# Tiles of SBUF moved to addresses that are multiples of 128 bytes, in a one-core attention and FFN layer

## The chip, the cores and the metric

One core of one Trainium2 chip runs the whole layer in one launch. The metric is the device time of that core in microseconds. TensorE (PE) multiplies, VectorE (DVE), ScalarE (ACT) and GpSimd (POOL) do the rest, and all transfers are issued by SyncE (SP). Working data lies in SBUF, where a tile has 128 partitions and the same byte range in each of them; "address" below means the first byte of that range. Matrix products land in PSUM.

## The reference, cut to what matters

One layer over 1,024 latent tokens and 256 context tokens, width 1,024, all in float32: modulated RMS norm, one input projection, two attention mixers that read the same input, one output projection, and a SwiGLU FFN of hidden width 2,816.

```
h  = _modulate(_rms_norm(x, norm1_g), sh1, sc1);  hc = _modulate(_rms_norm(ctx, norm1_g), csh1, csc1)
q_a, k_a, v_a, q_b, k_b, v_b = _in_proj(h, w_in)          # and the same for hc
o_a = _window_gqa_latent(q_a, k_a, v_a, k_ac, v_ac, sink_a)
o_b = _neighbourhood_latent(q_b, k_b, v_b, k_bc, v_bc, rpb_b)
x_new = x + g1 * _merge(o_a, o_b, on_a, on_b, w_out)
h2 = _modulate(_rms_norm(x_new, norm2_g), sh2, sc2)
x  = x_new + g2 * ((silu(h2 @ w_gate) * (h2 @ w_up)) @ w_down)
```

## The kernel before, in words

Every large product is made of three matmuls, since each operand is split into a high part (the value rounded to float32r, written by ACT) and a low part (the rest, by DVE or POOL): high times high, high times low, low times high, summed in one PSUM tile. One operand of a matmul is the moving one (512 columns here, 2,048 bytes of each partition), the other the stationary one (128 columns, 512 bytes), loaded into PE ahead of the matmul.

The stages, in order of time:

- **Input projection** (`gemm_k`, lines 246 to 248). Moving: the split weights `whi`, `wlo`. Stationary: the split input, `hTh` and `hl` for the eight latent row blocks, `hcTh` and its own `hl` tiles for the two context blocks. Key and value columns come first, the queries are mixed into the attention.
- **Attention A and B** (`scores`, `a_front`, `a_back`, `b_front`, `b_back`): score matmuls at line 452, softmax on DVE, ACT and POOL (line 494 scales the weights `P` by `den`), transposes at lines 506 and 636, copies of them into `PT` by ACT (lines 511, 641) and DVE (509, 639). The **output projection** is spread over B (`out_proj`, lines 809 to 811; moving `wo`, stationary `oh` and `ol`).
- **FFN, gate and up** (`group`, `prod`, lines 977, 979, 980). A 2x2 block scheme with seven products. Stationary: the split weight combinations `fwhl`. Moving: one of seven split combinations of the activations, `B11`, `B21`, `BT3`, `BT1`, `BT2`, `B22`, `BT4`, each with a high and a low tile (`h`, `l` at the end of the name).
- **FFN, down** (`dprod`, `dmm`, line 1188). Both operands are `dhl` tiles, of which there are 24; ACT and DVE split them from `draw` tiles just loaded (lines 114 and 117).

Each engine runs its instructions in the order in which the built program has them. Tiles come from pools. A pool lies at the left end of SBUF, behind the pools still open there, or (`side="right"`) at the right end, in front of the pools open there. Within a pool the tiles follow each other in the order of their first use, each rounded up to a multiple of 32 bytes. So one small tile moves everything behind it in its pool, and everything on the far side of its pool.

The left end begins at byte 1,152: 1,024 bytes that `kernel` sets aside (`dynamic_dma_scratch_size=1024`) and four constants of 32 bytes. The first left pool is `cons`, with the constants. It is released after the output projection, so that the pool `f1b` (with `BT1`, `BT2`, `B22`, `BT4`) and later `dn` (with `dhl`) start at 1,152. The right end is at byte 229,344. The pool `h` (`hTh`, then the `hl` tiles) ends there, and later the FFN's pool `fw`, in front of which stand `f1a` (`B11`, `B21`, `BT3`) and `fwh` (`fwhl`).

Of the kernel before, what the change touches and what calls it, by code (L numbers as in the profile page):

```python
# [5 lines left out]
F32 = mybir.dt.float32  # L6
# [7 lines left out]
D = 1024  # L14
SEQ = 1024
CTX = 256
HD = 64
# [31 lines left out]
XTE = (0, 2)  # L49
KTE = (0,)  # L50
WOG = (0, 2)
TEN = "GVV"


# [4 lines left out]
def block(tc, d, out, dbg=()):  # L59
# [4 lines left out]
    def pool(name, bufs=1, space=None, side=None):  # L64
        kw = {}
        if space is not None:
            kw["space"] = space
        if side is not None:
            kw["side"] = side
        return tc.alloc_tile_pool(name=name, bufs=bufs, reuse_waits="tile", **kw)  # L70


    cons = pool("cons")
    ident = cons.tile([128, 128], F32, name="ident")
    load(ident, d["ident"])
    ones = cons.tile([128, 128], F32, name="ones")
    V.memset(ones, 1.0)
    mhalf = cons.tile([128, 8], F32, name="mhalf")
    V.memset(mhalf, -0.5)
    col = cons.tile([128, 72], F32, name="col")  # L80
# [2 lines left out]
    sh1 = cons.tile([128, 8, 2], F32, name="sh1")  # L83
    a2 = cons.tile([128, 8], F32, name="a2")
    sh2 = cons.tile([128, 8], F32, name="sh2")
    g1 = cons.tile([128, D], F32, name="g1")
    sr = cons.tile([128, SEQ], F32, name="sr")
    rs = cons.tile([128, 2, 8], F32, name="rs")
    sink = cons.tile([128, 8], F32, name="sink")
    load(sink, d["sink_a"].to_broadcast([128, 8]))  # L90
    nsink = cons.tile([128, 8], F32, name="nsink")
    V.tensor_scalar(nsink, sink, -1.0, None, ALU.mult)

    dram = pool("scratch", space=DRAM)
# [8 lines left out]
    f_d = dram.tile([7, NJ // 2, 128, 512], F32, name="f_d")  # L103
    t_d = dram.tile([4, NJ // 2, 128, 512], F32, name="t_d")

    def rstd_of(p, ss, n, k, name):
        r = p.tile([128, k], F32, name=name, bufs=2)
        G.tensor_scalar(r, ss, 1.0 / n, EPS, ALU.mult, ALU.add)
        G.tensor_tensor(r, r, mhalf[:, :k], op=ALU.pow)
        return r  # L110
# [13 lines left out]
    def low(p, k, dt, name):  # L124

        if p < 2:
            return hp.tile([128, 512], dt, name=name, tag="hl", bufs=HLB)
        return hcp.tile([128, CTX], dt, name=name, tag="hcl", bufs=9)
# [25 lines left out]
    wk = pool("wk0", bufs=3, side="right")  # L154
# [5 lines left out]
    T.transpose(pcol[:, :72], vrow, ident[:72, :72])  # L160
    V.tensor_copy(col, pcol[:, :72])
    S.activation(sil, col[:, 0:16], AF.Silu)
    bsc = cons.tile([128, 8], F32, name="bsc")
    V.tensor_scalar(bsc, col[:, 24:32], 1.0, None, ALU.add)
    silw = wk.tile([128, 8, 32], F32, name="silw", bufs=1)
    V.memset(silw, 0.0)
    V.tensor_copy(silw[:, :, 0:2], sil.rearrange("p (s k) -> p k s", s=2))
    sel = wk.tile([128, 2], F32, name="sel", bufs=1)
    load(sel, d["sel"])

    xT = {}
# [1 line left out]
    def load_x(i):  # L173
        xt = wk.tile([128, D], F32, name=f"x{i}", tag="in", bufs=XB)
        load(xt, d["x"][i * 128:(i + 1) * 128] if i < 8 else d["ctx"][(i - 8) * 128:(i - 7) * 128])
        ss = wk.tile([128, 1], F32, name="ss")
        S.activation(sr, xt, AF.Square, accum_out=ss)
        r = rstd_of(wk, ss, D, 1, "rx")
        V.tensor_scalar(xt, xt, r, None, ALU.mult)
        p, m = divmod(i, 4)  # L180
        if m == 0:
            xT[p] = [low(p, k, F32, f"xT{p}{k}") for k in range(8)]
        for half in range(2):
            pt = ps1.tile([128, 512], F32, name="ptx", tag="tr", bufs=2)
            for c in range(4):
                T.transpose(pt[:, c * 128:(c + 1) * 128],
                            xt[:, (4 * half + c) * 128:(4 * half + c + 1) * 128], ident)
            for c in range(4):
                dst = xT[p][4 * half + c][:, m * 128:m * 128 + 128]
                if c in XTE:  # L190
                    V.tensor_copy(dst, pt[:, c * 128:(c + 1) * 128])
                else:
                    S.activation(dst, pt[:, c * 128:(c + 1) * 128], AF.Copy)
# [65 lines left out]
        for m in range(NF):  # L259
            gemm_k(pgs[m], m, dd, ws[dd], 512)  # L260

    gkb = cons.tile([128, 2, HD], F32, name="gkb")
    for j, nm in enumerate(("qn_b", "kn_b")):
        load(gkb[:, j], d[nm].to_broadcast([128, HD]))
    V.scalar_tensor_tensor(gkb[:, 0], gkb[:, 0], 0.125, gkb[:, 1], ALU.mult, ALU.mult)
# [3 lines left out]
    for c in XO:  # L269
        if c < 10:  # L270
            load_x(c)
            if c == 3:
                h_kb(0)
            continue
        mods(c - 10)
        if c > 10:
            h_kb(c - 10)
# [165 lines left out]
    at = pool("at", bufs=2)  # L443

    def scores(segs, lh, ll):
        s = psA.tile([128, 1024], F32, name="s", tag="s", bufs=2)
        for n_, l in enumerate((lh, ll)):
            for o, rhs, n in segs:
                ov = s[:, o:o + n]
                if len(rhs.shape) == 3:  # L450
                    ov = ov.rearrange("p (r c) -> p r c", c=rhs.shape[2])
                T.matmul(ov, l, rhs, start=n_ == 0, stop=n_ == 1)  # L452
        return s

    def geo(i):
        b0, b1 = max(i - 1, 0), min(i + 1, 7)
        nl = (b1 - b0 + 1) * 128
        if i == 7:
            return b0, nl, 512, 256, 256, 0, [8, 9] + list(range(b0, b1 + 1))
        return b0, nl, 512 - nl, 512, 512 - nl, 256 + 384 - nl, list(range(b0, b1 + 1)) + [8, 9]  # L460
# [9 lines left out]
    def a_front(i, g, Ps, QT):  # L470
        QTh, QTl = QT
        b0, nl, lo_o, cx_o, s0, m0, blocks = geo(i)
        n = nl + CTX
        nm = at.tile([128, 4], F32, name="nm", bufs=3)
        den = at.tile([128, 4], F32, name="den", bufs=3)
        for h in range(4):
            hh = 4 * g + h
            s = scores([(lo_o, KTa[:, g, b0 * 128:b0 * 128 + nl], nl),
                        (cx_o, KTa[:, g, SEQ:SEQ + CTX], CTX)],
                       QTh[:, h * 128:(h + 1) * 128], QTl[:, h * 128:(h + 1) * 128])  # L480
            P = at.tile([128, 640], F32, name="P", bufs=10)
            V.tensor_tensor_reduce(P[:, :n], s[:, s0:s0 + n], mska[:, m0:m0 + n], -1.0,  # L482
                                   nsink[:, hh:hh + 1], ALU.add, ALU.min, nm[:, h:h + 1])
            S.activation(P[:, :n], P[:, :n], AF.Exp, scale=-1.0, bias=nm[:, h:h + 1],  # L484
                         accum_out=den[:, h:h + 1])
            Ps.append(P)
            yield
        es = at.tile([128, 4], F32, name="es", bufs=3)
        V.tensor_tensor(es, nm, sink[:, 4 * g:4 * g + 4], op=ALU.add)
        S.activation(es, es, AF.Exp)  # L490
        V.tensor_tensor(den, den, es, op=ALU.add)
        V.reciprocal(den, den)  # L492
        for h in range(4):
            G.tensor_scalar(Ps[h][:, :n], Ps[h][:, :n], den[:, h:h + 1], 1.0, ALU.mult, ALU.mult)  # L494
# [100 lines left out]
    def b_front(hp_, C, Ps, QT, bias):  # L595
        QTh, QTl = QT
        KT = kvs[hp_]
        nm = atb.tile([128, 4], F32, name="nm", bufs=3)
        den = atb.tile([128, 4], F32, name="den", bufs=3)
        for R in range(2):  # L600
            r0 = 4 * R
            for h in range(2):
                j = 2 * R + h
                kl = KT[h][:, :SEQ].rearrange("p (r c) -> p r c", c=64)[
                    :, r0:r0 + 12, C0S[C]:C0S[C] + 32]
                kc = KT[h][:, SEQ:]
                if R == 0:
                    s = scores([(256, kc, 256), (512, kl, 384)], QTh[:, j], QTl[:, j])
                    s0, m0 = 256, 384
                else:  # L610
                    s = scores([(128, kl, 384), (512, kc, 256)], QTh[:, j], QTl[:, j])
                    s0, m0 = 128, 0
                P = atb.tile([128, 640], F32, name="P", bufs=PBB)
                V.tensor_tensor_reduce(P, s[:, s0:s0 + 640], bias[h][:, m0:m0 + 640], -1.0,  # L614
                                       3.0e38, ALU.add, ALU.min, nm[:, j:j + 1])
                S.activation(P, P, AF.Exp, scale=-1.0, bias=nm[:, j:j + 1],  # L616
                             accum_out=den[:, j:j + 1])
                Ps.append(P)
                yield
        V.reciprocal(den, den)  # L620
        for j in range(4):
            G.tensor_scalar(Ps[j], Ps[j], den[:, j:j + 1], 1.0, ALU.mult, ALU.mult)  # L622
# [94 lines left out]
    for u in range(16):  # L717
# [18 lines left out]
        if u == UR:  # L736
# [3 lines left out]
            atb = pool("at2", bufs=2, side="right")  # L740
# [35 lines left out]
    def load_wo(grp):  # L776
        ws = []
        for c in range(4):
# [6 lines left out]
            r = col[:, 64 + 4 * grp + c:65 + 4 * grp + c]  # L785
            if c in WOG:
                G.tensor_scalar(raw, raw, r, 1.0, ALU.mult, ALU.mult)
# [124 lines left out]
    fw = pool("fw", side="right")  # L912
# [2 lines left out]
    ones2 = fw.tile([128, 128], F32, name="ones2", bufs=1)  # L915
    V.memset(ones2, 1.0)
    acc2 = fw.tile([128, 512], F32, name="acc2", bufs=1)
    sil2 = fw.tile([128, 8], F32, name="sil2", bufs=1)
    V.tensor_copy(sil2, sil[:, 0:8])
    B = {}  # L920
    for nm_ in ("11", "21", "T3"):
# [206 lines left out]
    E = {"V": V, "G": G}  # L1128
    TE = [E[x] for x in TEN]
    for k in range(4):  # L1130
# [125 lines left out]
    dn.release()  # L1256
    fw.release()
    psT.release()
    dram.release()


# [89 lines left out]
```

## Time and profile before

| | |
|---|---|
| three runs | 1409.66, 1413.19, 1413.55 us; median 1413.19 us |
| the profiled execution's own time | 1412.19 us |
| its span (first to last instruction) | 1410.4 us, so 1.8 us lie outside |
| mean granted TensorE clock | 0.975 |
| busy: PE, DVE, POOL, ACT | 1318.8, 935.8, 615.3, 598.1 us |
| transfers | 250.20 MB in 192,228 packets, 177 GB/s over the span |

Times are microseconds from the first instruction, means of one instruction are nanoseconds. A matmul's duration includes its way through the pipelined array, so that matmuls of 390 ns follow each other every 0.23 us: the rate is read from the starts. After "idle before" stands how long the engine stood idle just before instructions of that group, and what ended it.

### The profile page before, as it was taken

The page shows a single profiled execution, that of the slowest core. Times are in us where ns is not written, and L with a number is a line of the kernel's source. Part 1 is how long each engine was busy: PE and PEld are TensorE (multiplying, and loading weights), DVE is VectorE, ACT ScalarE, POOL GpSimd, SP SyncE. Part 2 cuts the span into 40 slices and gives each one's busy share as a digit, 9 for nine tenths or more (in the row PEclk, how much of TensorE's full clock was granted, in tenths as well). Part 3 has the DMA queues.
Part 4 walks back from the last instruction along what each step waited for, and adds up shares of the span by engine and source line. Part 5 has one row for each costly group of instructions (what it writes and reads, how often), then busy time and mean ns, then how long its engine had stood idle before and what let it go on. Part 6 is the DMA issues. An engine that isn't in the chain of part 4 may idle for free. (4 is left out here: it accounts for less than half of the span.)

```text
span 1410.4 us, 19052 instructions
## 1 busy us (share of the span) xinstructions
PE 1318.8 (94%) x6537; PEld 1020.5 (72%) x6537; DVE 935.8 (66%) x1533; ACT 598.1 (42%) x1200; POOL 615.3 (44%) x541
## 2 busy tenths in 40 slices
PE   6989988999998799999987889999999997999998
PEld 3668866766655477677765678888888886888886
DVE  4687775577555555566558877867777764857762
ACT  4555323554455444455644423333333331744430
POOL 1377555342122434565435686666666753000000
PEclk8999999999998899999989999999999999999999
DMA  9635364265236865556386355555555443975832
GB/s 278 212 133 196 99 171 100 73 187 186 90 99 191 218 216 188 208 166 216 112 239 217 112 189 178 175 170 169 179 187 179 156 165 129 388 281 198 279 105 59
DMA packets 192228, 250.20 MB, mean 177 GB/s; under 512 B 44604, under 2 KB 115460, under 8 KB 192004
## 3 DMA queue, kind: packets, MB, share of 16 engines
q1 hardware_dynamic: 192132, 248.99, 55.6%
q8 instruction: 51, 0.84, 0.3%
q14 instruction: 45, 0.37, 0.1%
HBM read 182.10 MB, written 66.85 MB: 177 GB/s over the span
## 5 line engine op out<-in xcount | busy, mean ns | idle before, releaser
L1188 PE MATMUL pf<-dhl 128*128 128x512 f32 x924 | 212.1, 392 | 7.1 <-DVE dhl L117 7.1
L1188 PEld LDWEIGHTS pf<-dhl 128*128 128x128 f32 x924 | 175.0, 189 | 44.1 <-DVE dhl L117 7.6
L248 PE MATMUL pg<-whi,hl 128*128 128x512 f32 (+1 forms) x368 | 134.9, 378 | 1.8 <-POOL hl L117 1.8
L117 DVE TENSOR_TENSOR dhl<-draw,dhl 128x512 fp32r<-128x512 f32 x154 | 101.8, 707 | 49.5 <-ACT dhl L114 49.4
L114 ACT ACTIVATE dhl<-draw 128x512 fp32r<-128x512 f32 x154 | 87.9, 624 | 107.2 <-PE pf L1188 75.4
L246 PE MATMUL pg<-whi,hTh 128*128 128x512 f32 (+1 forms) x320 | 122.9, 384 | 7.8 <-ACT qc L323 6.5
L117 DVE TENSOR_TENSOR fwhl<-fs,fwhl 128x512 fp32r<-128x512 f32 x88 | 101.2, 1159 | 37.6 <-ACT fwhl L114 35.2
L247 PE MATMUL pg<-wlo,hTh 128*128 128x512 f32 (+1 forms) x320 | 121.3, 379 | 0.0
L494 POOL TENSOR_SCALAR P<-P,den 128x640 f32<-128x640 f32 (+1 forms) x64 | 51.6, 827 | 119.3 <-DVE den L492 74.4
L939 POOL TENSOR_TENSOR fs<-fraw 128x512 f32<-128x512 f32 x44 | 62.5, 1424 | 78.9 <-DMA fraw<-in_w_up_dram 32.1
L248 PEld LDWEIGHTS pg<-whi,hl 128*128 128x128 f32 x368 | 69.8, 191 | 14.3 <-POOL hl L117 2.5
L114 ACT ACTIVATE fwhl<-fraw 128x512 fp32r<-128x512 f32 x58 | 36.7, 632 | 100.1 <-PE pf L980 98.4
L114 ACT ACTIVATE fwhl<-fs 128x512 fp32r<-128x512 f32 x88 | 54.8, 626 | 55.8 <-PE pf L980 54.2
L246 PEld LDWEIGHTS pg<-whi,hTh 128*128 128x128 f32 x320 | 61.2, 191 | 21.3 <-ACT qc L323 8.1
L117 DVE TENSOR_TENSOR fwhl<-fraw,fwhl 128x512 fp32r<-128x512 f32 x58 | 71.5, 1233 | 0.7 <-ACT fwhl L114 0.3
L622 POOL TENSOR_SCALAR P<-P,den 128x640 f32<-128x640 f32 x64 | 51.5, 825 | 43.9 <-DVE den L620 28.5
L247 PEld LDWEIGHTS pg<-wlo,hTh 128*128 128x128 f32 x320 | 61.3, 192 | 9.5
L484 ACT ACTIVATE P<-P,nm 128x640 f32<-128x640 f32 (+1 forms) x64 | 51.0, 798 | 39.8 <-DVE nm L482 39.7
L482 DVE CUSTOM_DVE_ANT_0 P<-s,mska,nsink 128x640 f32<-128x640 f32 (+1 forms) x64 | 52.4, 846 | 18.3 <-PE s L452 16.1
L813 POOL TENSOR_TENSOR xa<-xa,xt 128x512 f32<-128x512 f32 x28 | 40.8, 1461 | 47.2 <-DVE xa L812 38.6
L616 ACT ACTIVATE P<-P,nm 128x640 f32<-128x640 f32 x64 | 52.7, 825 | 16.1 <-DVE nm L614 16.0
L506 PEld LDWEIGHTS pt<-ident,P 128*128 128x128 f32 x304 | 34.0, 141 | 31.1 <-issue 24.4
(296 smaller groups left out, 3451.9 us busy)
## 6 DMA issues: line engine op xcount, KB each, us to landing
draw<-f_d SPq DMA_DIRECT2D x35, 512.0 KB
bt<-in_bias_b_dram SPq DMA_DIRECT2D x16, 1024.0 KB
wraw<-in_w_mod_dram SPq DMA_DIRECT2D x48, 256.0 KB
fraw<-in_w_gate_dram SPq DMA_DIRECT2D x22, 512.0 KB
fraw<-in_w_up_dram SPq DMA_DIRECT2D x22, 512.0 KB
wr<-in_w_down_dram SPq DMA_DIRECT2D x22, 512.0 KB
f_d<-sc SPq DMA_DIRECT2D x44, 256.0 KB
t_d<-wt SPq DMA_DIRECT2D x44, 256.0 KB
```

The lines of the kernel that those rows point to most:

```text
L114: S.activation(hi, src, AF.Copy)
L117: lo_eng.tensor_tensor(lo, src, f(hi), op=ALU.subtract)
L246: T.matmul(pg[:, :n], l, w[0][:, :n], start=k == 0, stop=False)
L247: T.matmul(pg[:, :n], l, w[1][:, :n], start=False, stop=False)
L248: T.matmul(pg[:, :n], hl[m // 4, k][:, m % 4 * 128:m % 4 * 128 + 128], w[0][:, :n], start=False, stop=k == 7)
L482: V.tensor_tensor_reduce(P[:, :n], s[:, s0:s0 + n], mska[:, m0:m0 + n], -1.0, nsink[:, hh:hh + 1], ALU.add, ALU.min, nm[:, h:h + 1])
L484: S.activation(P[:, :n], P[:, :n], AF.Exp, scale=-1.0, bias=nm[:, h:h + 1], accum_out=den[:, h:h + 1])
L494: G.tensor_scalar(Ps[h][:, :n], Ps[h][:, :n], den[:, h:h + 1], 1.0, ALU.mult, ALU.mult)
L616: S.activation(P, P, AF.Exp, scale=-1.0, bias=nm[:, j:j + 1], accum_out=den[:, j:j + 1])
L622: G.tensor_scalar(Ps[j], Ps[j], den[:, j:j + 1], 1.0, ALU.mult, ALU.mult)
L939: G.tensor_tensor(t, x, y, op=op_)
L1188: T.matmul(pd[t], a[:, x, l], b[:, y], start=start and i == 0, stop=stop and i == 2, skip_group_check=True)
```

## The change

The first part is a 96-byte pool that is opened on the right before all others and released last. `EDGE` is 24 float32. The second part reorders the constants, so that the large ones (`ident`, `ones`, `g1`, `sr`, `gkb`) come before the small ones; `bsc` and `gkb` move up to the others, and `nsink` takes 64 bytes. The third part pads small tiles in the other pools (`sel`, `ss`, `rx`, `nm`, `den`, `es`, `sil2`) to 128 or 64 bytes, and instructions use the first columns.

```diff
+EDGE = 24
...
+    edge = pool("edge", side="right")
+    edge.tile([128, EDGE], F32, name="edge")
     cons = pool("cons")
     ident = cons.tile([128, 128], F32, name="ident")
     load(ident, d["ident"])
     ones = cons.tile([128, 128], F32, name="ones")
     V.memset(ones, 1.0)
+    g1 = cons.tile([128, D], F32, name="g1")
+    sr = cons.tile([128, SEQ], F32, name="sr")
+    gkb = cons.tile([128, 2, HD], F32, name="gkb")
...
-    nsink = cons.tile([128, 8], F32, name="nsink")
+    bsc = cons.tile([128, 8], F32, name="bsc")
+    nsink = cons.tile([128, 16], F32, name="nsink")[:, :8]
...
-    def rstd_of(p, ss, n, k, name):
-        r = p.tile([128, k], F32, name=name, bufs=2)
+    def rstd_of(p, ss, n, k, name, room=8):
+        r = p.tile([128, room], F32, name=name, bufs=2)[:, :k]
...
-    sel = wk.tile([128, 2], F32, name="sel", bufs=1)
+    sel = wk.tile([128, 32], F32, name="sel", bufs=1)[:, :2]
...
-        ss = wk.tile([128, 1], F32, name="ss")
+        ss = wk.tile([128, 32], F32, name="ss")[:, :1]
         S.activation(sr, xt, AF.Square, accum_out=ss)
-        r = rstd_of(wk, ss, D, 1, "rx")
+        r = rstd_of(wk, ss, D, 1, "rx", 16)
...
-        nm = at.tile([128, 4], F32, name="nm", bufs=3)
-        den = at.tile([128, 4], F32, name="den", bufs=3)
+        nm = at.tile([128, 32], F32, name="nm", bufs=3)[:, :4]
+        den = at.tile([128, 32], F32, name="den", bufs=3)[:, :4]
...
-    sil2 = fw.tile([128, 8], F32, name="sil2", bufs=1)
+    sil2 = fw.tile([128, 32], F32, name="sil2", bufs=1)[:, :8]
...
     psT.release()
+    edge.release()
     dram.release()
```

No instruction is added, removed or moved: on all five engines the built program has the same instructions in the same order, and only addresses and a few waits differ. The waits follow from addresses, since a new tile waits for whatever used its bytes last. On ACT one write of `whi` loses a wait for a transfer and the first write of `BT1h` a wait for ACT itself. On POOL four writes of `wlo` wait for other earlier users, and one scaling of `P` (line 494, 512 columns) waits for PE besides ACT.

Of the 2,097 allocations of SBUF in the built program, 502 lie at a multiple of 128 before, and 2,016 after; the other 81 are small ones (`hss`, `hr`, `rx`, `xss` and constants). For the operands of the 512-column matmuls, this is where they lie, as the address modulo 512 bytes. Each slice of an operand steps by a multiple of 512 bytes, so one number stands for all of its slices.

```
pair (moving, stationary)             line            before       after        distance: before, after
whi/wlo, hTh and its hl               246 to 248      352, 480     256, 384     128   128
whi/wlo, hcTh and its hl              246 to 248      352, 352     256, 384       0   128
wo, oh/ol                             809 to 811      352, 352     384, 384       0     0
B11/B21/BT3, fwhl                     977, 979, 980   448, 448     256, 256       0     0
BT1/BT2/B22/BT4, fwhl                 977, 979, 980   128, 448     128, 256     320   128
dhl, dhl                              1188            128, 128     128, 128       0     0
```

The distance is stationary minus moving, modulo 512. Modulo 128 the distances of the six pairs are 0, 0, 0, 0, 64, 0 before and all 0 after.

## Rows read from the trace of the kernel before

**Rows 1.** The page's head: busy time of each engine, share of the span, instructions.
```profile
span 1410.4 us, 19052 instructions
PE 1318.8 (94%) x6537; PEld 1020.5 (72%) x6537; DVE 935.8 (66%) x1533; ACT 598.1 (42%) x1200; POOL 615.3 (44%) x541
```
**Rows 2.** Busy time by stretch; columns: length, PE, PEld, DVE, ACT, POOL, clock, DMA share, GB/s.
```profile
0.00:35.00 35.00, 21.62 (x123) 13.79 (x124) 15.43 (x44) 15.43 (x38) 5.29 (x14) 0.85 0.97 278
126.00:412.00 286.00, 273.83 (x1425) 204.62 (x1424) 185.87 (x412) 122.44 (x275) 118.20 (x134) 0.99 0.43 124
412.00:726.00 314.00, 287.90 (x1747) 211.85 (x1746) 178.52 (x373) 154.67 (x331) 137.35 (x144) 0.96 0.63 192
726.00:1184.00 458.00, 438.54 (x1866) 349.91 (x1867) 339.73 (x360) 161.56 (x278) 290.69 (x192) 0.99 0.52 171
1184.00:1410.00 226.00, 212.58 (x927) 175.17 (x926) 146.99 (x227) 91.81 (x163) 8.24 (x5) 0.98 0.63 220
```
**Rows 3.** Timeline of PE, down stage: start, length, engine, line, tiles, count.
```profile
1209.74 30.54 PE L1188 MATMUL pf<-dhl 128*128 128x512 f32 x134
```
**Rows 4.** Timeline of PE, FFN: first matmul of each k-run, one per row.
```profile
1000.52 0.39 PE L977 MATMUL pf<-B21h,fwhl 128*128 128x512 f32 x1
...
1001.90 0.39 PE L977 MATMUL pf<-B21h,fwhl 128*128 128x512 f32 x1
...
1003.26 0.39 PE L977 MATMUL pf<-B22h,fwhl 128*128 128x512 f32 x1
...
1006.06 0.39 PE L977 MATMUL pf<-BT4h,fwhl 128*128 128x512 f32 x1
...
1008.86 0.39 PE L977 MATMUL pf<-B11h,fwhl 128*128 128x512 f32 x1
```
**Rows 5.** Timeline of PE, input projection: context blocks, then latent blocks.
```profile
93.04 0.40 PE L248 MATMUL pg<-whi,hl 128*128 128x512 f32 x1
93.28 0.40 PE L246 MATMUL pg<-whi,hcTh 128*128 128x512 f32 x1
...
108.18 0.39 PE L248 MATMUL pg<-whi,hl 128*128 128x512 f32 x1
...
113.62 0.39 PE L248 MATMUL pg<-whi,hl 128*128 128x512 f32 x1
...
193.09 0.39 PE L248 MATMUL pg<-whi,hl 128*128 128x512 f32 x1
...
199.85 0.40 PE L247 MATMUL pg<-wlo,hTh 128*128 128x512 f32 x1
```
**Rows 6.** Groups by line and form: matmuls of the FFN and of the context blocks.
```profile
L1188 PE MATMUL pf<-dhl 128*128 128x512 f32 x924 | 212.1, 392 | 7.1 <-DVE dhl L117 7.1
L977 PE MATMUL pf<-BT4h,fwhl 128*128 128x512 f32 x88 | 34.8, 395 | 3.7 <-DVE p L1086 3.7
L979 PE MATMUL pf<-B22l,fwhl 128*128 128x512 f32 x88 | 34.7, 394 | 0.0
L980 PE MATMUL pf<-B21h,fwhl 128*128 128x512 f32 x88 | 34.3, 389 | 0.0
L246 PE MATMUL pg<-whi,hcTh 128*128 128x512 f32 x32 | 13.3, 415 | 3.1 <-ACT qc L323 3.1
```
**Rows 7.** Groups by line and form: copies into PT, in attention A and B.
```profile
L641 ACT ACTIVATE PT<-pt 128x512 f32<-128x512 f32 x48 | 28.5, 594 | 49.3 <-PE pt L636 49.2
L511 ACT ACTIVATE PT<-pt 128x512 f32<-128x512 f32 x44 | 26.2, 595 | 52.9 <-PE pt L506 52.9
L509 DVE COPY PT<-pt 128x512 f32<-128x512 f32 x32 | 22.0, 687 | 26.0 <-PE pt L506 26.0
L639 DVE COPY PT<-pt 128x512 f32<-128x512 f32 x32 | 21.9, 686 | 11.5 <-PE pt L636 11.3
```
**Rows 8.** Groups by line and form: POOL instructions whose waits differ.
```profile
L494 POOL TENSOR_SCALAR P<-P,den 128x512 f32<-128x512 f32 x16 | 11.8, 760 | 13.6 <-ACT P L484 7.9 <-DVE den L492 5.7
L117 POOL TENSOR_TENSOR wlo<-wraw,whi 128x512 fp32r<-128x512 f32 x16 | 22.8, 1437 | 6.7 <-ACT whi L114 6.6
```

More of the change, by code (lines that the diff above doesn't have):

```diff
@@ L85, in block @@
     sh2 = cons.tile([128, 8], F32, name="sh2")
-    g1 = cons.tile([128, D], F32, name="g1")
-    sr = cons.tile([128, SEQ], F32, name="sr")
     rs = cons.tile([128, 2, 8], F32, name="rs")
@@ L162, in block @@
     S.activation(sil, col[:, 0:16], AF.Silu)
-    bsc = cons.tile([128, 8], F32, name="bsc")
     V.tensor_scalar(bsc, col[:, 24:32], 1.0, None, ALU.add)
@@ L260, in h_kb @@
             gemm_k(pgs[m], m, dd, ws[dd], 512)
-    gkb = cons.tile([128, 2, HD], F32, name="gkb")
     for j, nm in enumerate(("qn_b", "kn_b")):
@@ L487, in a_front @@
             yield
-        es = at.tile([128, 4], F32, name="es", bufs=3)
+        es = at.tile([128, 32], F32, name="es", bufs=3)[:, :4]
         V.tensor_tensor(es, nm, sink[:, 4 * g:4 * g + 4], op=ALU.add)
@@ L597, in b_front @@
         KT = kvs[hp_]
-        nm = atb.tile([128, 4], F32, name="nm", bufs=3)
-        den = atb.tile([128, 4], F32, name="den", bufs=3)
+        nm = atb.tile([128, 32], F32, name="nm", bufs=3)[:, :4]
+        den = atb.tile([128, 32], F32, name="den", bufs=3)[:, :4]
         for R in range(2):
```

## The prediction

> **What bounds the kernel now.** I read the head of the page first: PE is busy for 1318.8 of 1410.4 us, and no other engine is above 66% [rows 1]. The split by stretch then tells where this holds. In the FFN's gate and up stage PE is busy for 438.54 of 458 us, in the down stage for 212.58 of 226, in the stretch of projections and attention from 126 to 412 us for 273.83 of 286, from 412 to 726 us for 287.90 of 314; only the first 35 us belong to the transfers, with a DMA share of 0.97 against 21.62 us of PE [rows 2]. A busy PE is not yet PE at its peak, so the third view is PE's timeline, for the rate at which matmuls start. The reader should see that one shape, 128x512, starts at two rates at a granted clock of 0.98 to 0.99, the 2.4 GHz level.
>
> **Two rates.** In the down stage 134 matmuls take 30.54 us; less 0.39 us for the last one's pipeline this is 30.15 over 133 intervals, 226.7 ns [rows 3]. In the FFN the twelve matmuls with `B22` and the twelve with `BT4` start from 1003.26 to 1008.86 us: 5.60 us over 24, 233.3 ns. Just before, the last six with `B21` take from 1001.90 to 1003.26: 226.7 ns; the first six take 1.38 us, 230 ns [rows 4]. Same line, same weights, no wait: only the moving tile differs, and with it the address. `B21` lies at distance 0 from `fwhl` modulo 512, `B22` and `BT4` at 320.
>
> The input projection gives the third case. The context blocks (distance 0) run 24 intervals from 108.18 to 113.62 us, 226.7 ns; the latent blocks (distance 128) run 29 from 193.09 to 199.85 us, 233.1 ns [rows 5]. So in these rows a pair at distance 0 settles at 226.7 ns, and pairs at 320 and at 128 both run at about 233. That the pair at 128 is slow is the row to hold on to: modulo 128 its distance is already 0.
>
> **The change part by part.** It adds no instruction, so every term is an old one at a new address. Each is worked out against the profiled execution's 1412.19 us, which is 1.0 us below the median of the runs.
>
> 1. *FFN, the four pairs `BT1`, `BT2`, `B22`, `BT4`.* 4 names x 3 lines x 88 = 1056 matmuls [rows 6]. Their distance goes from 320 to 128. No row shows distance 128 in this stage. The bounds are 226.7 ns (the fast rate of rows 3 to 5) and 240 ns (the slowest start-to-start step at distance 128, from 93.04 to 93.28 us [rows 5]). That is 1056 x -6.6 = -7.0 us to 1056 x +6.7 = +7.1 us. I take 233.1, the latent blocks' mean, since they are the only pair in the trace with this very distance: 1056 x -0.2 = **-0.2 us**. PE is the bound of this stage, so the term counts in full.
> 2. *Context blocks.* Their distance goes from 0 to 128. With 512 columns these are 32 matmuls at each of three lines [rows 6], 96 in all, from 226.7 to 233.1 ns: **+0.6 us**. Bounds 0 and 96 x 13.3 = +1.3 us. Part of it lies in front of waits for ACT's `qc` (3.1 us of idle before them), so 0.6 is rather too much.
> 3. *Pairs whose distance stays.* Latent blocks (128), `dhl` (924 matmuls, 0), `B11`, `B21`, `BT3` (792 matmuls, 0), `wo` with `oh` and `ol` (0). **0.** If they change after all, it is by their slow start behind another pair, 230 instead of 226.7 ns over six matmuls, 20 ns each time [rows 4]; at 66 runs this bounds the term at 1.3 us either way.
> 4. *ACT, DVE and POOL.* `PT` lies at a multiple of 128 in attention A and 96 past one in B. ACT writes it in 595 and 594 ns, DVE in 687 and 686 [rows 7]: one part in 600, in favour of neither. **0.** What hides even that is the wait for the transposes (49.2 to 52.9 us of ACT's idle); without that cover, 1 ns x 156 copies is 0.2 us.
> 5. *Transfers.* Only where DMA is the bound can this count, in the first 35 us with 278 GB/s at a share of 0.97 [rows 2]. Per unit of share that is 287 GB/s, against 220/0.63 = 349 in the down stage. If the whole difference came from addresses, the 35 us would shrink by 6 us; I see no row in which it does, and the first stretch has other packet sizes. I take **0**, with -1.5 us (a quarter of that bound) as what could come unseen, and nothing above 0, because no transfer gets a longer run or a later place in its queue. Later transfers hide under PE.
> 6. *Waits.* Four `wlo` writes on POOL and one `P` scaling get other waits. The engine's idle time before these groups is ended by ACT or DVE and not by PE or a transfer (6.6 of 6.7 us, and 7.9 + 5.7 of 13.6 us) [rows 8]; an extra wait on something already done costs nothing. One `P` scaling that did wait would hold up three more of 0.76 us. **0**, bounds -0.5 and +1. The two waits lost on ACT stood beside ones that stay.
>
> Sum: 1412.19 - 0.2 + 0.6 = **1412.6 us**.
>
> **A page of the Trainium skill that speaks against the change.** At 32-byte multiples every tile already starts on a whole line of the 16 bytes that the Trainium skill names ("SBUF — State Buffer", Operand start alignment and Door 1), and the page calls start alignment a matter of legality, not of speed. By that page terms 1 and 2 are 0 and the sum is 1412.2 us. The trace agrees with it for ACT and DVE [rows 7], but not for PE, whose two rates the page does not know [rows 4, 5].
>
> **Rivals.**
>
> *A. The distance counts modulo 128, not modulo 512.* Then the change brings every pair to 0, and the 1056 matmuls of term 1 run at 226.7 ns: -7.0 us. The slow starts behind a changed pair go too, 66 x 0.02 = -1.3 us, and term 2 is 0. Result 1403.9 us. For it: 320 is 64 modulo 128, and all pairs seen at 226.7 ns are 0 modulo 128. Against it: the latent blocks, 0 modulo 128 and slow for as long as they run. A could only hold if these are slow for another reason, such as their place far to the right in SBUF, where `hTh` and its `hl` are the only stationary operands of such matmuls.
>
> *B. At distance 128 the FFN settles above 233 ns.* The trace has steps of 240 ns at this distance, at the end of the latent blocks [rows 5], while at 320 no such scatter is seen. If the FFN's four pairs ran at 239, the price is 1056 x 5.7 = +6.0 us, with term 2 1418.8 us. It decides from 4 ns on: 1056 x 4 = 4.2 us. Against it: over 29 steps such values are balanced by shorter ones.
>
> *C. Addresses do nothing on PE; the rate hangs on which ends of SBUF the two operands lie at.* `BT1`, `BT2`, `B22` and `BT4` lie left and `fwhl` right, `dhl` both left, and the change moves no tile across. Then the change is one in name only: 1412.2 us. Against it: latent blocks, where both operands lie right, are slow.
>
> **How the numbers follow.** Three runs of this kernel spread over 3.9 us, so 0.3% (4.2 us) is about what a measurement tells from no change: the borders are 1409.0 and 1417.4 around the median. My forecast has 0.60, A 0.22, B 0.10, C 0.08. The forecast's own range is 1409.5 to 1415.5; I count 0.03 of it beyond either border, from terms 1 and 5 and the spread. Faster: 0.22 + 0.03 = 0.25. Slower: 0.09 of B (it ends beyond the border unless it is half as large) + 0.03 = 0.12. Same: 0.63. For 8 in 10 the range has to hold the forecast, C and most of A: from 1403.0 us, just under A's 1403.9, to 1417.0, which leaves out the upper part of B.
>
> **What the profile afterwards would show.** Right: `B22` and `BT4` with `fwhl` still start about every 233 ns, twelve matmuls in 2.80 us; the context blocks now take 233 instead of 226.7; `dhl` stays at 226.7; ACT and DVE means for `PT` stay within 2 ns. Wrong by A: twelve `B22` matmuls in 2.72 us, and the stage from the first FFN matmul to the first of line 1188 shorter by 7 to 8 us. Wrong by B: steps of 237 ns and more that don't balance. Wrong in a way I have no row for: other means on POOL, or a shorter first 35 us.

## The result, and the profile after the change

| | before | changed |
|---|---|---|
| median | 1412.21 us (4 runs, 1409.66 to 1413.55) | 1404.59 us (4 runs, 1401.26 to 1404.87) |
| ratio | | 0.9943, 95% interval [0.9921, 0.9964] |
| the profiled execution's own time | 1412.19 us | 1404.77 us |
| its span and mean granted clock | 1410.4 us, 0.975 | 1403.0 us, 0.978 |

The time lies in the forecast range of 1403.0 to 1417.0, but the forecast was no change (1412.6 us) and the kernel is 0.57% faster. By the prediction's own border of 1409.0 us this is "faster", which it gave a chance of 0.25. It even lies near rival A's 1403.9 us. The profile shows that it got there by another way.

First the rates on PE, which carried most of the prediction. The timeline of PE in the FFN of the changed kernel, one matmul of several k-runs (start, length, engine, line, tiles, count):

```profile
994.83 0.39 PE L980 MATMUL pf<-B21h,fwhl 128*128 128x512 f32 x1
...
996.19 0.40 PE L980 MATMUL pf<-B22h,fwhl 128*128 128x512 f32 x1
...
998.98 0.40 PE L980 MATMUL pf<-BT4h,fwhl 128*128 128x512 f32 x1
...
1001.78 0.39 PE L980 MATMUL pf<-B11h,fwhl 128*128 128x512 f32 x1
```

`B22` and `BT4` take 5.59 us for 24 matmuls, 232.9 ns each (233.3 before, [rows 4]); the last six with `B21` take 1.36 us, 226.7 ns. The context blocks and the down stage, in the same view:

```profile
92.62 0.40 PE L252 MATMUL pg<-whi,hl 128*128 128x512 f32 x1
...
95.42 0.40 PE L252 MATMUL pg<-whi,hl 128*128 128x512 f32 x1
...
1199.64 40.73 PE L1191 MATMUL pf<-dhl 128*128 128x512 f32 x179
```

Twelve matmuls of a context block now take 2.80 us, 233.3 ns (226.7 before, [rows 5]). `dhl` stays at (40.73 - 0.39)/178 = 226.6 ns [rows 3]. So every rate came out as forecast, and rival A's 226.7 ns in the FFN did not appear.

Now the time by stretch. Kernel before, then the changed one (columns as in [rows 2]):

```profile
412.00:495.00 83.00, 65.22 (x371) 45.02 (x371) 46.12 (x101) 40.95 (x85) 23.70 (x25) 0.86 0.72 205
```
```profile
0.00:35.00 35.00, 21.06 (x147) 13.82 (x148) 15.29 (x44) 16.62 (x41) 6.20 (x14) 1.00 0.92 301
...
412.00:495.00 83.00, 68.29 (x405) 47.37 (x403) 48.10 (x105) 42.65 (x89) 28.76 (x31) 0.92 0.80 228
```

The first 35 us move 301 instead of 278 GB/s at a smaller share, and PE gets through 147 instead of 123 matmuls [rows 2]. From 412 to 495 us it gets through 405 instead of 371.

PE runs the same 6,537 matmuls in the same order in both kernels, so the start of each can be compared. Worked out in this way, the changed kernel is ahead by 2.9 us at 140 us, 5.4 at 350, 11.25 at 500, 11.2 at 700, only 6.7 at 820, and 7.4 at the end, which is the difference of the two spans. The times are those of the kernel before. So there are three places: a gain at the start, a gain at the start of attention B, and a loss at the start of the FFN. (The second profile of this kernel, further below, doesn't repeat the 2.5 us between 140 and 350 us: there it is 0.2.)

What ends PE's waits from 412 to 500 us (line, waited for: us in all, times, longest). Kernel before, then the changed one:

```profile
PE pt L556 <- DMA kkb<-kb_d: 6.3, 2, 4.1
PE pg L809 <- DVE oh L116: 4.8, 1, 4.8
PE pt L556 <- DVE KTb L561: 3.9, 1, 3.9
```
```profile
PE pg L812 <- DVE oh L121: 4.7, 1, 4.7
PE pt L559 <- DMA kkb<-kb_d: 3.8, 1, 3.8
PE pt L559 <- DVE KTb L564: 3.1, 2, 2.9
```

Before the change the largest of these in sum was a wait for a transfer, `kkb`, with which attention B begins. It is 2.5 us shorter now, and the wait for `KTb` at 481 us, 1.0 us. The remaining 2.4 of the 5.9 us between 350 and 500 us accrue while PE in the kernel before runs at the lower level of its granted clock (1.2 of 2.4 GHz): 23.9 us in this stretch against 13.7 in the changed kernel. One of these drops, at 446 us before and at 444 us after, begins just behind a wait for `kkb`.

SP's queue shows why `kkb` came earlier. Its timeline, kernel before, then the changed one:

```profile
420.99 5.86 SPq L589 DMA_DIRECT2D vp<-vb_d  x4
...
442.93 4.58 SPq L551 DMA_DIRECT2D kkb<-kb_d  x3
```
```profile
415.33 4.46 SPq L592 DMA_DIRECT2D vp<-vb_d  x4
...
435.58 4.10 SPq L554 DMA_DIRECT2D kkb<-kb_d  x3
```

From the first `vp` issue to the first of the three `kkb` issues SP takes 20.25 instead of 21.94 us, and the three `kkb` issues themselves 4.10 instead of 4.58. So `kkb` is issued and lands earlier. At the very start the transfers' rate shows it. The head of the transfer view from 12 to 28 us, while `wm` and `wraw` are loaded; DMA is busy nearly throughout in both (kernel before, then changed):

```profile
DMA packets 6922, 5.25 MB, mean 328 GB/s; under 512 B 290, under 2 KB 6044, under 8 KB 6922
```
```profile
DMA packets 7660, 5.73 MB, mean 358 GB/s; under 512 B 318, under 2 KB 6703, under 8 KB 7660
```

### The profile page after: what moved, and what is told of

Read it like the earlier page. It is cut to its first block, busy times and chain, and to the rows that moved or that the text cites. A ratio compares the mean times of both kernels' runs of the same rounds, so it can differ in the third digit from the quotient of the medians.

```text
span 1403.0 us, 19050 instructions
## 1 busy us (share of the span) xinstructions
PE 1316.0 (94%) x6537; PEld 1020.0 (73%) x6537; DVE 932.1 (66%) x1533; ACT 598.3 (43%) x1200; POOL 620.6 (44%) x541
## 5 line engine op out<-in xcount | busy, mean ns | idle before, releaser
L942 POOL TENSOR_TENSOR fs<-fraw 128x512 f32<-128x512 f32 x44 | 65.5, 1495 | 80.3 <-DVE fwhl L122 54.2
L122 DVE TENSOR_TENSOR fwhl<-fraw,fwhl 128x512 fp32r<-128x512 f32 x58 | 67.5, 1164 | 0.6
```

The source lines that it names most:

```text
L122: lo_eng.tensor_tensor(lo, src, f(hi), op=ALU.subtract)
L942: G.tensor_tensor(t, x, y, op=op_)
```

## The experiments

Theory T: a transfer takes longer when its tile in SBUF doesn't start at a certain multiple of bytes, and PE's start and the start of attention B wait for such transfers. Rivals: A (distances on PE count modulo 128) and L (PE's clock drops merely fell elsewhere). Every pad in `wk` or `atb` below stands at the end of a pool on the right, and so moves that pool's other tiles, and what is opened in front of it, by its own size. `wk` has `x` and `wm`; `atb` has `kkb`, `bt`, `qdb` and `vp`.

### Each pool put back, and each moved alone

Back, in the changed kernel:

```diff
+    wk.tile([128, 16], F32, name="wkpad", bufs=1)
     wk.release()
```

> The changed kernel with the input stage's tiles (x, wm, hf and the small ones) moved back to 64 past a multiple of 128, where x and wm lay before; all else stays. Theory T (transfers): the first 75 us lose the 3.1 us that they gained, the 512-byte packets into wm go from 27 back to about 32 ns, and the whole takes 1407 to 1408 us. Rival A (matmul pairs): no large matmul moves against its partner, so 1404.6. Rival L (the clock's drops fall elsewhere by chance): anything within 3 us, with packets as fast as in the changed kernel.

```diff
+    atb.tile([128, 24], F32, name="atbpad", bufs=1)
     atb.release()
```

> The changed kernel with the tiles of attention B (kkb, bt, qdb, vp, KTb, PT) moved back to 32 past a multiple of 128. Theory T: the stretch in which attention B's first transfers come in (about 410 to 490 us) loses the 5.8 us that it gained, so 1409 to 1410 us, unless the FFN's start gives a part of it back. Rival A: 1404.6. Rival L: within 3 us either way, and the transfers into vp issue as fast as in the changed kernel.

Alone, in the kernel before (48 columns in `wk`, or 40 in `atb`):

```diff
+    wk.tile([128, 48], F32, name="wkpad", bufs=1)
     wk.release()
```

> The kernel before with only the input stage's tiles moved, so that x and wm start at a multiple of 128; nothing else moves. Theory T: the first 75 us are 3 us shorter, the whole 1409 us against 1412.2. Rival A: no change, 1412.2. Rival L: no change beyond 2 us.

```diff
+    atb.tile([128, 40], F32, name="atbpad", bufs=1)
     atb.release()
```

> The kernel before with only attention B's tiles moved to a multiple of 128. Theory T: the stretch from 410 to 490 us is up to 5.8 us shorter, and the whole 1407 to 1410 us, since the FFN's start gives some back. Rival A: no change, 1412.2. Rival L: no change beyond 2 us.

Measured against 1415.60 us for the kernel before on that chip: `wk` back 1408.72 us, ratio 0.9948 [0.9929, 0.9967]; `atb` back 1409.20, 0.9958 [0.9941, 0.9974]; `wk` alone 1411.26, 0.9968 [0.9956, 0.9980]; `atb` alone 1410.94, 0.9968 [0.9951, 0.9985]. Each part alone gives a gain that A has no place for, since neither touches an FFN pair. Whether undoing one part costs time can't be told from these intervals, which overlap the changed kernel's, nor from the ends of the profiles (`wk` back is 3.4 us ahead there, the changed kernel 7.4 and, in a second profile, 3.5); the stretches tell it. The first 35 us with `wk` back and with `wk` alone (columns as in [rows 2]):

```profile
0.00:35.00 35.00, 19.62 (x142) 12.46 (x142) 15.51 (x44) 15.86 (x39) 5.85 (x14) 1.00 0.97 281
```
```profile
0.00:35.00 35.00, 21.26 (x149) 13.94 (x149) 15.28 (x44) 16.73 (x42) 6.20 (x14) 1.00 0.94 306
```

281 against 306 GB/s. In both the granted clock is 1.00, so L's reading of the 0.85 before [rows 2] falls here: with `wk` back the clock stays up and PE is all the same only 0.2 us ahead of the kernel before at 140 us. What it waits for `wm` from 10 to 45 us, with `wk` back and with `wk` alone:

```profile
PE pr L213 <- DMA wm<-in_w_mod_dram: 3.9, 5, 1.3
```
```profile
PE pr L209 <- DMA wm<-in_w_mod_dram: 1.9, 4, 0.9
```

In the kernel before this wait is 1.7 us, as in the changed one; there the time goes while PE runs at the lower clock, 10.2 of the first 35 us.

The wait for `kkb` with `atb` back is nearly that of the kernel before, and its three issues take 4.55 us again. (The four `vp` issues don't follow the address: 4.74 us here and 4.38 with `wk` alone, both at 32, against 4.25 to 4.97 at 128. So their 5.86 before can't be put down to it.)

```profile
PE pt L559 <- DMA kkb<-kb_d: 5.8, 2, 4.3
```

### Both pools alone, and the changed kernel again

The first kernel is the one before with the two pads (48 columns in `wk`, 40 in `atb`), the second the changed kernel unaltered.

> The kernel before with two pads alone: 192 bytes in wk (x, wm to 0 modulo 256) and 160 in atb (kkb, bt, qdb, vp to 128 modulo 256). Edge, constants and all other tiles stay as before, so the FFN's four pairs stay at distance 320. If the transfers into these two pools are the whole effect of the change: ratio 0.994, within 2 us of the changed kernel that runs beside it. If the other tiles that were moved have a share (transfers of attention A or of the FFN, ACT or DVE at other addresses): 2 us or more above the changed kernel, 0.9955 or higher.

> The changed kernel unaltered, on the same chip as the other three of this call: ratio 0.994, and a second profile, to see how far its schedule scatters. What is the change's and not scatter should be in both profiles: a first 35 us of 300 to 307 GB/s, about 3 us gained by 130 us, 3 to 6 more between 350 and 490 us, and a part of it given back between 714 and 820 us.

The two pads: 1406.76 us, ratio 0.9941 [0.9917, 0.9964]. The changed kernel beside it: 1406.13 us, 0.9936 [0.9914, 0.9957]. So the two pools are the whole effect, as far as these intervals tell (some 3 us either way). The second profile of the changed kernel also shows the scatter of one profile: it is ahead by 3.2 us at 140 us, by 3.4 at 350, by 6.7 at 500 (the first by 11.25) and by 3.5 at the end; its own time, 1408.67 us, is the slowest of its six.

### Is it 128 or 256?

In the changed kernel, 32 more columns in `atb` (to 0 modulo 256), or 32 in `wk` (to 128 modulo 256):

```diff
+    atb.tile([128, 32], F32, name="atbpad", bufs=1)
     atb.release()
```

> The changed kernel with another 128 bytes in pool atb: kkb, bt, qdb and vp go from 128 to 0 modulo 256. Two forms of the transfer theory part here. If a multiple of 128 is all that counts: nothing changes, the four vp transfers at the start of attention B are issued in about 4.5 us and the three kkb ones in 4.1 as in the changed kernel, time within 1 us of it. If a multiple of 256 counts: these issues get shorter again (by the 0.4 to 1.4 us that the step from 32 to 128 modulo 128 gave, or more), PE's schedule at 490 us gains up to another 5 us, and the time is 1 to 4 us lower after what the start of the FFN gives back.

```diff
+    wk.tile([128, 32], F32, name="wkpad", bufs=1)
     wk.release()
```

> The changed kernel with 128 bytes more in pool wk: x and wm go from 0 to 128 modulo 256 (in the kernel before they lie at 64 modulo 128). If a multiple of 128 is all that counts for a transfer: the first 35 us move 301 to 306 GB/s at a share of 0.92 to 0.94 as in the changed kernel, and the time is the same. If a multiple of 256 counts: 278 to 285 GB/s at 0.97, about 3 us lost by 130 us and a time 1 to 4 us above the changed kernel, as with the pool put back by 64.

Against 1415.27 us: `atb` at 0 modulo 256 takes 1399.77 us, ratio 0.9904 [0.9881, 0.9928]; `wk` at 128 modulo 256 takes 1407.56 us, 0.9949 [0.9930, 0.9969]. For `wk`, 128 is worth nothing: the first 35 us are those of the kernel before.

```profile
0.00:35.00 35.00, 20.70 (x129) 13.25 (x133) 15.62 (x44) 15.58 (x38) 5.78 (x14) 0.95 0.96 281
```

For `atb`, 0 modulo 256 gives about as much again by the profiles; by the times the interval still overlaps the changed kernel's a little. SP's timeline:

```profile
435.93 3.72 SPq L554 DMA_DIRECT2D kkb<-kb_d  x3
```

What PE waits for from 412 to 500 us:

```profile
PE pt L559 <- DMA kkb<-kb_d: 2.5, 1, 2.5
```

Over all 14 profiles (those of the next section too), grouped by where the two pools lie modulo 256. "Ahead" is PE's schedule against the kernel before, by the matmuls' starts:

```
wk at     kernels   GB/s, 0 to 35 us   ahead at 140 us
192       3         277 to 281         0 to 0.6
128       1         281                0.1
0         10        299 to 307         2.7 to 3.7

atb at    kernels   three kkb issues   PE's wait for kkb   gained, 350 to 500 us
32        3         4.44 to 4.58 us    5.2 to 6.3 us       0 to 1.9
128       8         3.95 to 4.17       3.6 to 4.1          3.3 to 5.9
0         3         3.72 to 3.78       1.5 to 3.6          5.9 to 8.2
```

For `wk`, 192 and 128 are alike and 0 stands apart. For `atb` the three groups don't overlap in the issues and hardly elsewhere. SP's time from the first `vp` issue to the first of the three `kkb` issues goes the same way: 20.9 to 21.9 us at 32, 19.9 to 20.6 at 128, 18.5 to 19.7 at 0. The wait itself is 2.2 to 2.7 us shorter in all eight kernels at 128 than before the change. The other 0.8 to 3.5 us that they gained come with shorter waits for `KTb` and with less time at the lower clock (13.7 to 20.5 us from 350 to 500 us, 23.9 before), so a share of the gain stays open to L. The pad in `atb` also moves tiles on which PE, ACT and DVE work, `KTb` and `PT` among them; but from 500 to 700 us, while attention B goes on with them, the leads change by no more than 1.3 us, up or down.

Packets, counted in the trace, go the same way for `wm`, whose pieces have 512 bytes: mean 31.2 to 32.1 ns at 192, 30.7 at 128, 27.1 to 27.2 at 0 modulo 256. For `kkb`, also 512 bytes, it is 30.1 ns at 32, 29.7 at 128 and 28.4 at 0 (means of the groups over the first twelve transfers). `x`, which lies in `wk` too and comes in pieces of 4 KB, shows no such step: 183 to 185 ns at 192, 179 to 186 at 0. And the 2-KB packets of `wraw`, which a pad in `wk` doesn't move, go along all the same: 93.0 ns in the kernel before, 84.6 with `wk` alone. So a packet's mean doesn't tell of its own tile's address alone.

The Trainium skill ("DMA: Bandwidth & Descriptors", How a descriptor splits into AXI transactions) says that a descriptor's piece which starts off a multiple of 256 is rounded down to one, and that the bytes in front are fetched for nothing and paid for in beats of 32. The Trainium skill tells this of reading. By that rule of the Trainium skill, laid on the tile that is written, as an estimate, 512 bytes need 22 beats at 192, 20 at 128 and 16 at 0. The order agrees with `wm`; the size doesn't, since 32.1/27.2 is 1.18 and not 22/16. At 32 the rule counts 17 beats, fewer than at 128, and there the runs say otherwise: the `kkb` issues take longer at 32 than at 128, with packets about equal.

### Distances on PE

In the changed kernel, 128 bytes between the pools `fw` and `f1a`; `fwhl`, `B11`, `B21`, `BT3` come to 128 modulo 512, and all FFN pairs to distance 0:

```diff
+    shim = pool("shim", side="right")
+    shim.tile([128, 32], F32, name="shim")
     f1a = pool("f1a", side="right")
...
     dn.release()
+    shim.release()
     fw.release()
```

> The changed kernel with 128 bytes set aside between the FFN's right-hand pools, so that fwhl and B11, B21, BT3 come to 128 modulo 512, where BT1, BT2, B22, BT4 already lie: every pair of the FFN is now at distance 0. Nothing else moves. If the rate of a pair hangs on its distance modulo 512: the 1056 matmuls with BT1, BT2, B22 and BT4 start every 226.7 instead of 233 ns, 1056 x -6.2 = -6.5 us, and the slow starts of the other three go, up to -1.1 us: 6 to 8 us below the changed kernel, ratio to the kernel before about 0.989. If only the distance modulo 128 counts (rival A): all these pairs are at 0 either way, no change, ratio 0.994. If the place in the left or right end of SBUF counts (rival C): no change either.

1400.55 us against 1415.27, ratio 0.9899 [0.9878, 0.9919]. The same view as above:

```profile
996.83 0.39 PE L982 MATMUL pf<-B22h,fwhl 128*128 128x512 f32 x1
...
999.55 0.39 PE L982 MATMUL pf<-BT4h,fwhl 128*128 128x512 f32 x1
...
1002.27 0.39 PE L982 MATMUL pf<-B11h,fwhl 128*128 128x512 f32 x1
```

24 matmuls in 5.44 us: 226.7 ns. From 820 to 1180 us its PE schedule gains 6.2 us on the changed kernel's. That was the forecast of the distance modulo 512; A and C, which expected no change, fall.

The same for the input projection: 384 bytes between the pools `h` and `ip` bring `whi` and `wlo` to 384 modulo 512, where `hTh`, `hcTh` and `hl` lie.

```diff
+    shim2 = pool("shim2", side="right")
+    shim2.tile([128, 96], F32, name="shim2")
     ip = pool("ip", bufs=2, side="right")
...
+    wk.tile([128, 32], F32, name="wkpad", bufs=1)
     wk.release()
...
             ip.release()
+            shim2.release()
```

> The changed kernel with 384 bytes set aside in front of the split input's pool (and 128 in wk, which keeps x and wm at a multiple of 256), so that whi and wlo come to 384 modulo 512, where hTh, hcTh and hl lie: the input projection's pairs go from distance 128 to 0. By the distance modulo 512: 864 matmuls of 512 columns, 5 to 6 ns each, -4 to -5 us, part of which may be lost in waits for transfers and for ACT before the FFN; ratio to the kernel before about 0.991. By rival A or C: ratio 0.994, and the latent blocks still start every 233 ns.

1402.99 us, ratio 0.9917 [0.9895, 0.9940]. The rate did what was expected (228.5 instead of 232.5 ns between starts, worked out over all undisturbed ones), the time hardly. PE waits longer for ACT's `qc`: 11.1 us from 40 to 412 us, where it was 8.7. Its profile is ahead of the changed kernel's by 0.8 us at 140 us and behind by 1.2 at 350. By the medians the gain is not to be told from none.

### A version faster than both

All pads together (32 columns in `atb`, 32 in `wk`, 96 in `shim2`), with the FFN's 128 bytes behind `fw` (first) or in front of it (second), where it also brings `hin`, `fah`, `fraw`, `sg` and `gw` to 0 modulo 256:

```diff
+    shim = pool("shim", side="right")
+    shim.tile([128, 32], F32, name="shim")
     fw = pool("fw", side="right")
...
     fw.release()
+    shim.release()
```

> The changed kernel with the three pads that helped put together: fwhl and B11, B21, BT3 at distance 0 from the other four (shim between pools fw and f1a), whi and wlo at distance 0 from the split input, atb at 0 modulo 256. By the sum of the single steps: FFN -6.5, input projection -1 to -3 (the part that is not lost in waits for qc), attention B -4: 11 to 13 us below the changed kernel, ratio to the kernel before 0.985 to 0.987. If one step takes away what the other gives (the next wait is the same): 0.988 to 0.990.

> As e11_dist0_atb256, but with the 128 bytes in front of pool fw instead of behind it: the pairs lie at the same distances, and the FFN's transfer tiles hin, fah, fraw, sg, gw and draw go from 128 to 0 modulo 256 besides. If transfers into these tiles bind PE at the start of the FFN as they did at the start of attention B: the eight hin issues (12.2 us in the changed kernel) get shorter by 1 us or more, and the time is 1 to 4 us below e11. If they lie under PE: equal to e11 within 1.5 us.

1394.23 us, ratio 0.9850 [0.9827, 0.9874], and 1393.54 us, 0.9847 [0.9823, 0.9870], against 1414.64. The second is 21.1 us below the kernel before and 12.6 below the changed one beside it. Its head:

```profile
span 1393.5 us, 19050 instructions
...
PE 1302.7 (93%) x6537; PEld 1016.3 (73%) x6537; DVE 938.0 (67%) x1533; ACT 598.8 (43%) x1200; POOL 617.0 (44%) x541
```

The steps add up to what was forecast for the first version (11.9 us below the changed kernel), and the two versions are equal: the same 128 bytes that were worth several us in `atb` are worth nothing in `fw`. That the FFN's transfers lie under PE is not shown by this, because they didn't get shorter. The eight `hin` issues, first version and second:

```profile
696.01 11.22 SPq L937 DMA_DIRECT2D hin<-h_d  x8
```
```profile
693.10 12.53 SPq L937 DMA_DIRECT2D hin<-h_d  x8
```

Pieces of `hin` have 2 KB, and over the 14 profiles these issues take 10.1 to 13.0 us without regard to the address.

### The loss at the start of the FFN

No run isolates this; the 14 profiles tell how far it goes. The clock there, by stretch, in the kernel before, the changed one and `atb` at 0 modulo 256:

```profile
710.00:820.00 110.00, 87.76 (x348) 66.23 (x349) 89.68 (x109) 47.17 (x84) 60.95 (x42) 0.92 0.62 188
```
```profile
710.00:820.00 110.00, 87.90 (x339) 66.15 (x338) 93.83 (x109) 49.99 (x89) 66.08 (x44) 0.89 0.58 194
```
```profile
710.00:820.00 110.00, 90.00 (x351) 68.34 (x352) 92.43 (x109) 47.77 (x85) 68.23 (x45) 0.92 0.56 183
```

The time from 700 to 820 us that the granted clock was at its lower level (1.2 of 2.4 GHz) goes with what a kernel gives back of its lead there:

```
at the lower level      17.1 us   20.5 us     23.9 us      27.3 us
other profiles          2         4           4            3
gives back, mean        0.5 us    2.3 us      2.3 us       4.3 us
```

The kernel before is at 17.1. From the first column to the last, 10.2 us more at half speed go with 3.8 us lost; half of 10.2 would be 5.1. The drop at 717 us begins in the second of PE's first two waits for `fwhl` (2.01 and 2.56 us), the one at 726 us before the change in the first (2.55 and 2.08). Why the drops are longer and more in some profiles stays open.

## Why the prediction was right, and where it was wrong

**Terms 1 to 3 were right.** The four FFN pairs start every 232.9 ns where I took 233.1, the context blocks every 233.3, and pairs whose distance stayed kept their rate. The distance modulo 512, read from one row of latent blocks at distance 128 [rows 5], was the right reading, and e5 shows it as a cause. Term 1 itself came out near its -0.2 us: from 820 to 1180 us the changed kernel gains 0.7 us in both profiles, and the three kernels with the old addresses in the FFN gain none.

**Term 4 was right.** ACT writes `PT` in 593 ns in attention B, as before [rows 7]:

```profile
L644 ACT ACTIVATE PT<-pt 128x512 f32<-128x512 f32 x48 | 28.5, 593 | 50.5 <-PE pt L639 50.4
```

**Term 6 was right** as far as it can be seen: the `P` scaling on POOL has the same mean and the same idle time, ended by ACT and DVE [rows 8].

```profile
L497 POOL TENSOR_SCALAR P<-P,den 128x512 f32<-128x512 f32 x16 | 11.8, 758 | 13.6 <-ACT P L487 7.9 <-DVE den L495 5.8
```

**Term 5 was the step that failed**, in its two sentences. "Only where DMA is the bound can this count, in the first 35 us": there it did count, 2.7 to 3.7 us by 140 us in the ten profiles with `wk` at 0, inside its bound of 6 and above the 1.5 that I allowed to come unseen. The 287 GB/s per unit of share, which I had in front of me, became 301/0.92 = 327. "Later transfers hide under PE": at the start of attention B they don't. PE stood 6.3 us there for `kkb` before the change, and the moves gained 3.3 to 5.9 us between 350 and 500 us, 2.2 to 2.7 of them at this wait. The sentence had no row of PE's waits behind it. The DMA share that I had for this stretch (0.63 from 412 to 726 us [rows 2]) is a mean over a start in which PE waits for a transfer and a long rest in which it doesn't. Against the kernel's own sum, about 3 and 4.4 us (mean of the eight profiles) came from these two places, and up to 4.5 went back at the start of the FFN, for which the prediction has no term.

**The rivals.** A gave nearly the right time, 1403.9 us, by a mechanism that isn't there. Its chance of 0.22 is what brought the range down to where the result fell, so the range held by luck, for a wrong reason. B did not appear: at distance 128 the four pairs' means are 232.9 to 233.7 ns, and it needed 237. C falls with e5, which moves no tile across and gains.

**The page of the Trainium skill** that I set against the change ("SBUF — State Buffer", Operand start alignment) says of its rule on the start that it is about legality, not speed, and that its runs timed nothing. That a start costs no time was my reading and not the page's word. In these rows it costs none on ACT and DVE (`PT`), but it does on transfers: `wm` packets of 27.2 against 32.1 ns.

## What to carry to other kernels

Before you cost a move of transfers at nothing, ask in each stretch what ends the bounding engine's waits, and price every wait that a transfer ends; a mean DMA share hides a stage's first microseconds. Try multiples of 256 bytes for tiles that transfers of 512-byte pieces fill, above all those that a stage waits for first; the 2-KB pieces of `hin` and the 4-KB pieces of `x` showed nothing. And give the two operands of a float32r matmul the same address modulo 512. A predicted time that comes true says nothing on the mechanism until its own row is checked.

## What was not expected of the hardware

- A transfer's packets of 512 bytes take a different time by the tile's start modulo 256: 27.1 to 27.2 ns at 0, 30.7 at 128, 31.2 to 32.1 at 192 (`wm`). At 32 the issues of `kkb` are longer than at 128 (4.44 to 4.58 us against 3.95 to 4.17) although their packets are about equal; why stays open.
- 512-column float32r matmuls whose two operands lie at the same address modulo 512 start every 226.6 to 227.1 ns in the down stage and in an FFN whose pairs all lie so, every 228.5 in the input projection, and about every 229 in the output projection; at a distance of 128 or 320 they start every 232.5 to 233.7. Moving the tiles alone switches it.
- A part of a lead that PE gains can go back along with its own granted clock: 17.1 to 27.3 us at the lower level from 700 to 820 us, with no change in what it computes.
